# A two-layer streaming encoder: the first MLP's h tiles are issued from ScalarE's queue, and its loads, its side work and the norm behind it are paced differently

## The chip, the core and the metric

The kernel runs on one core of a Trainium2 chip. Its time is the device time of one launch in microseconds (us). Three runs of the kernel before gave 2468.64, 2472.65 and 2472.76 us; the median is 2472.65 us.

The engines are named as in the profile: PE is the matrix engine (TensorE), PEld its weight loads, DVE is VectorE, ACT is ScalarE, POOL is GpSimd, SP is the sync engine, which in this kernel issues the transfers (DMA). An engine works through its own instructions in the order in which they stand, and a transfer is issued when its turn comes on the engine that issues it.

## The reference

One inference step of a two-layer encoder, 1024 prompt tokens and 32 sample tokens side by side (T = 1056), width 1024, float32 throughout:

```
layer 0:  u = x*(1+sc1)+sh1;  y = mLSTM mixer(u);   x = LN(ALPHA*x + (1+g1)*y)
          u = x*(1+sc2)+sh2;  f = square(relu(u @ w_up[0])) @ w_down[0]      # the first MLP, 1024 -> 4096 -> 1024
          x = LN(ALPHA*x + (1+g2)*f)
layer 1:  kv = (x*(1+kv_scale)+kv_shift) @ w_kv;  q = (x*(1+sc1)+sh1) @ w_q
          y = band attention(q, k, v);  x = LN(ALPHA*x + (1+g1)*y);  second MLP;  LN
sh1,sc1,g1,sh2,sc2,g2 of a layer = silu(c) @ w_ada[layer] + b_ada       # "conditioning", 1024 -> 6*1024
kv_shift, kv_scale               = silu(c) @ w_ada_kv + b_ada_kv        # 1024 -> 2*1024
```

The conditioning vectors of layer 1 and of the shared keys and values depend on `c` alone, so they can be computed at any time before the second layer starts.

## The kernel before

Activations stand with features on the partitions and tokens along the free dimension. Every float32 operand of a matmul is split into a rounded part and a remainder: ScalarE casts (`split`, L89), VectorE subtracts (L90), and a product takes three matmuls (L118 to L120, or L1280 in a loop). The 1056 tokens are cut into four quarters of 264 for the up half of the first MLP and into blocks of 384, 384 and 288 (`TBS`) from there on.

**Up half.** `mlp7` with the class `L0` computes `h = square(relu(u @ w_up))` for 16 blocks `pb` of 256 columns. Ten of them (`FIRST`) are computed plainly for the first half of the tokens, while the norm ahead of the MLP still runs. The rest goes in 22 jobs `(pb, tp)` of seven products each (`Seven`, L1280): first blocks with both token halves and blocks with the second half in turn, and at the end five jobs in a row that each bring a new `pb`. For each `pb`, `forms` loads two 128x4x256 tiles `rdn_u` (L1228) and makes eight split operands `wf_u` with sums on VectorE (L1244 to L1247). The result of a job is split into `HL` and stored to the array `hpl` in DRAM (L1147). The loop sorts the products by `7*j+2*i`, and writes TensorE's order out by hand; on the other engines a scheduler places the instructions when the program is built, by its own estimate of when each could start.

**Down half.** Eight groups `g` of 512 rows of `w_down`. A group needs four `h` tiles (`h_load`) and four weight tiles (`w_plain`, 128x4x256 each, load at L96, split at L89 and L90 as `w_dn`), and adds 8 output chunks of 128 columns to the residual `ACX` on VectorE (`add_gated_at`, L1045). The `h` tiles of group 0 are eight strips (L1336) that are loaded into parts of `U` as soon as the last job that reads them is done; those of odd groups are in a pool `f4`, which takes the place of the pool of `H` and `HL`, and those of even groups in `U` again (L1340). The residual comes back from DRAM in four pieces (`reload`, L1620) into two buffers that held operands of the up half.

**Rings.** `raw` has 3 buffers: `rdn_u`, `raw_dn` and the conditioning loads `rada` go through it in turn. `wc` has 6 buffers: `wf_u`, `w_dn` and the wide conditioning loads `radw` go through it.

**Side work.** `Flow` holds generators that compute the conditioning and the norms. Each yields how long to wait, and `tick` counts that down: after each of the seven products by `264/320`, after each output chunk of down by `n/192`. `ada_cols` handles two chunks of 128 columns at a time from two `rada` loads (L231), `ada_wide` four from two `radw` loads (L261), with 16 operations on VectorE per unit of work (L238, L241; L274, L276), two transposes and two sums (L283, L285). During the up half `ada_some` computes all of `w_ada_kv`, during the down half `ada_rest` all of `w_ada[1]` and the table of the attention bias. Behind each block of the last group a norm starts (`norm`: sums L926 to L929, mean and variance on TensorE L923, centring L936, squares L938, L940, scale L951 to L955, modulation L370 to L375), whose result is the operand `U` of the projection `q` (copied out at L1672, L1673). `W01` are the waits between its steps.

## Time and profile before

| | |
|---|---|
| median of 3 runs | 2472.65 us (2468.64 to 2472.76) |
| the profiled execution, its own time | 2473.38 us |
| span of its trace | 2471.5 us |
| mean granted TensorE clock | 0.987 |
| busy: PE, PEld, DVE, ACT, POOL | 96%, 92%, 81%, 48%, 7% of the span |
| chain that ended last | PE 65%, DVE 15%, DMA 8%, ACT 4% |

The up half of the first MLP with its seven products ends at about 887 us of the span, the down half runs from about 881 to 1276 us, and the projection of `q` follows. Rows of the trace give the start in us, the duration in us, the engine, the line, the operation and its tiles; in brackets stands how long the engine stood idle just before, and what ended that. In a table by windows each engine has its busy time and its number of instructions, then come the granted clock of TensorE (1.00 is full speed), the mean busy share of the 16 transfer engines, and GB/s. In a grouped row the count stands after the x, then the busy time and the mean of one in ns, then the idle time before.

### The profile page before, as it was taken

Reading aid. Unit: us, or ns where it says so; the run is one execution under the profiler, and the core shown is the slowest. Engines: PE = TensorE matmul, PEld = TensorE weight load, DVE = VectorE, ACT = ScalarE, POOL = GpSimd, SP = SyncE. Lnnn points to the kernel's source line nnn. Section 1 sums busy time; section 2 is a strip of 40 time slices with the busy share of each in tenths; the row PEclk is TensorE's granted clock in tenths of the full one; section 3 lists DMA queues with packets and bytes.
Section 4 is the critical chain, followed back from the end, with each engine's and each line's share of the span. In section 5 each row is a group of like instructions: output and inputs, shape, how many; then the busy total and the mean of one; then the engine's idle time right before and its main releaser. Section 6 shows DMA issues by size and latency. Waiting matters only on the chain.

```text
span 2471.5 us, 44497 instructions
## 1 busy us (share of the span) xinstructions
PE 2371.9 (96%) x17180; PEld 2273.6 (92%) x17180; DVE 1993.4 (81%) x4254; ACT 1181.9 (48%) x2394; POOL 165.4 (7%) x315
## 2 busy tenths in 40 slices
PE   7999999999999879999999989999999999899997
PEld 4999999999999879999989977789999999899997
DVE  4899899788788889998487666754998888887778
ACT  4544456387566531001047457762776777322212
POOL 0211100000000000000000224420000000000003
PEclk9999999999999989999999999999999999999999
DMA  8433223436566895764422330032476779966642
GB/s 295 124 109 94 84 87 114 131 127 213 185 196 200 286 319 208 259 226 163 152 94 78 83 74 1 10 95 62 138 268 229 255 252 345 372 232 234 230 159 71
DMA packets 294264, 423.62 MB, mean 171 GB/s; under 512 B 15640, under 2 KB 225964, under 8 KB 288932
## 3 DMA queue, kind: packets, MB, share of 16 engines
q1 hardware_dynamic: 294052, 420.78, 50.9%
q8 instruction: 135, 2.21, 0.4%
q14 instruction: 77, 0.63, 0.1%
HBM read 304.91 MB, written 118.17 MB: 171 GB/s over the span
## 4 chain that ended last, share of the span: by engine, by line
PE 65%; DVE 15%; DMA 8%; ACT 4%; issue 3%; POOL 1%; SPq 0%; DVEq 0%; ACTq 0%; POOLq 0%
PE dn L1415 11%; PE up L1280 7%; PE dn L118 5%; PE dn L119 5%; PE dn L120 5%; PE pv L1849 3%; PE s L1792 2%; PE pt L1827 2%; DVE wf_u L90 2%; DMA rdn_u<-in_w_up_dram 2%; PE up L120 2%; PE up L118 2%; PE up L119 2%; DVE HL L90 1%; PE op_a L118 1%
## 5 line engine op out<-in xcount | busy, mean ns | idle before, releaser
L1045 DVE SCALAR_TENSOR_TENSOR ACX<-dn,ada,ACX 128x264 f32<-128x264 f32 (+6 forms) x664 | 281.8, 448 | 115.0 <-PE dn L120 68.6
L1415 PE MATMUL dn<-fx,wf_d 128*128 128x264 f32 x2016 | 254.2, 285 | 6.3 <-DVE ACX L1045 2.8
L1415 PEld LDWEIGHTS dn<-fx,wf_d 128*128 128x128 f32 x2016 | 248.7, 188 | 8.7 <-issue 2.6
L89 ACT CAST w_dn<-raw_dn 128x1024 fp32r<-128x1024 f32 x36 | 37.5, 1050 | 289.9 <-PE dn L120 131.8
L118 PE MATMUL dn<-hs,w_dn 128*128 128x384 f32 (+2 forms) x512 | 161.4, 315 | 0.7 <-DVE ACX L1045 0.7
L120 PE MATMUL dn<-hs,w_dn 128*128 128x384 f32 (+2 forms) x512 | 160.3, 313 | 1.3 <-DVE w_dn L90 1.3
L119 PE MATMUL dn<-hs,w_dn 128*128 128x384 f32 (+2 forms) x512 | 161.0, 315 | 0.0
L1280 PE MATMUL up<-U,wf_u 128*128 128x264 f32 x1056 | 145.8, 290 | 15.8 <-ACT wf_u L89 6.8
L1280 PEld LDWEIGHTS up<-U,wf_u 128*128 128x128 f32 x1056 | 136.2, 192 | 20.4 <-ACT wf_u L89 8.0
L1280 PE MATMUL up<-TF,wf_u 128*128 128x264 f32 x1056 | 142.9, 284 | 0.6 <-ACT H L1283 0.6
L1280 PE MATMUL up<-u,wf_u 128*128 128x264 f32 x1056 | 139.6, 285 | 1.2 <-ACT wf_u L89 0.6
L118 PE MATMUL dn<-U,w_dn 128*128 128x384 f32 (+2 forms) x416 | 130.8, 315 | 10.2 <-ACT w_dn L89 10.0
L1280 PEld LDWEIGHTS up<-TF,wf_u 128*128 128x128 f32 x1056 | 134.3, 188 | 0.9 <-ACT H L1283 0.8
L1280 PEld LDWEIGHTS up<-u,wf_u 128*128 128x128 f32 x1056 | 132.6, 188 | 1.9 <-ACT wf_u L89 0.8
L119 PE MATMUL dn<-U,w_dn 128*128 128x384 f32 (+2 forms) x416 | 130.9, 315 | 0.0
L120 PE MATMUL dn<-U,w_dn 128*128 128x384 f32 (+2 forms) x416 | 129.5, 313 | 0.0
L274 DVE SCALAR_TENSOR_TENSOR aw<-radw,cs,aw 128x512 f32<-128x512 f32 x168 | 118.9, 744 | 0.0
L238 DVE SCALAR_TENSOR_TENSOR ada_room<-ada_room,cs 128x256 f32<-128x256 f32 x224 | 99.7, 479 | 3.5 <-DMA ada_room<-in_w_ada_dram 3.5
L120 PEld LDWEIGHTS dn<-hs,w_dn 128*128 128x128 f32 x512 | 96.4, 188 | 1.7 <-DVE w_dn L90 1.7
L118 PEld LDWEIGHTS dn<-hs,w_dn 128*128 128x128 f32 x512 | 96.3, 188 | 1.1 <-DVE ACX L1045 1.0
L119 PEld LDWEIGHTS dn<-hs,w_dn 128*128 128x128 f32 x512 | 96.5, 188 | 0.0
L120 PE MATMUL up<-u,w_up 128*128 128x264 f32 x320 | 91.8, 288 | 4.2 <-DVE w_up L90 4.2
(394 smaller groups left out, 7187.3 us busy)
## 6 DMA issues: line engine op xcount, KB each, us to landing
hpl<-HL SPq DMA_DIRECT2D x144, 264.0 KB
rdn_u<-in_w_up_dram SPq DMA_DIRECT2D x64, 512.0 KB
hd<-HL SPq DMA_DIRECT2D x28, 1056.0 KB
fx<-hd SPq DMA_DIRECT2D x50, 528.0 KB
radw<-in_w_ada_dram SPq DMA_DIRECT2D x24, 1024.0 KB
hd<-HM SPq DMA_DIRECT2D x28, 792.0 KB
hs<-hpl SPq DMA_DIRECT2D x20, 1056.0 KB
raw_up<-in_w_up_dram SPq DMA_DIRECT2D x40, 512.0 KB
```

The costliest lines, as they stand in the source:

```text
L90: (eng or nc.vector).tensor_sub(dst_l, src, dst_h.bitcast(F32))
L118: nc.tensor.matmul(ps, wh, mov(0, k), start=(k == 0), stop=False)
L119: nc.tensor.matmul(ps, wh, mov(1, k), start=False, stop=False)
L120: nc.tensor.matmul(ps, wl, mov(0, k), start=False, stop=(k == nk - 1))
L238: nc.vector.scalar_tensor_tensor(acc[:, cnd], raw[:, k], sc, acc[:, cnd], op0=ALU.mult, op1=ALU.add)
L274: nc.vector.scalar_tensor_tensor(acc[cnd], raw[:, k], sc, acc[cnd], op0=ALU.mult, op1=ALU.add)
L1045: nc.vector.scalar_tensor_tensor(xs, ps[:, off + o:off + o + mm_], gate[:, fc, cnd:cnd + 1], xs, op0=ALU.mult, op1=ALU.add)
L1280: nc.tensor.matmul(p, self.ws[w][:, wl, k], moving(f, tp, xl, k), start=first and k + n_ == 0, stop=k == 3 and n_ == 2, skip_group_check=n ...
L1415: nc.tensor.matmul(p, ws[w][:, wl, k], t[:, s0, xl], start=first and k + n_ == 0, stop=k == kg - 1 and n_ == 2, skip_group_check=not first)
L1792: nc.tensor.matmul(s[:, b, :w], qst, kk[i][:, g, k0 + j0:k0 + j0 + w], start=(i == 0), stop=(i == 1))
L1827: nc.tensor.transpose(pt[:kp, j - j0, pr * P:(pr + 1) * P], ps_[pr][:, j * P:j * P + kp], ident)
L1849: nc.tensor.matmul(pv[64 * e:64 * e + 64, :nq], V[:kp, vt0 + j, g * 64:(g + 1) * 64], pts[e][:kp, j, :nq], start=(j == 0), stop=(j == nt - 1))
```

## The change

- `h_load` issues the full `h` tiles from ScalarE's queue instead of SP's. The strips stay on SP.
- The strips of group 0 are asked for twice per job (after products 2 and 5) instead of three times, over four jobs instead of three. The residual's pieces 0 and 1 come at job `lone + 5` and at the end of the up half instead of at jobs `lone + 2` and `lone + 3`; pieces 2 and 3 in group 0 instead of at the end of the up half. The `h` tiles of group 1 are asked for one per pair of chunks of group 0 instead of all four ahead of it.
- Conditioning: half of `w_ada_kv` (8 of 16 chunks) moves from `ada_cols` in the up half to `ada_wide` in the down half. The pace in the up half goes from 320 to 480, so the same waits last longer there. In the down half the waits of `ada_wide` go from 5, 5, 2 to 4.5, 4.5, 2, and what a tick overshoots is carried over to the next wait.
- The norm's waits behind the first two blocks get shorter, each block with its own.

```
-    def add(self, gen, wait=0.0, now=False):
-        self.tasks.append([gen, next(gen) if now else wait])
+    def add(self, gen, wait=0.0, now=False, carry=False):
+        self.tasks.append([gen, next(gen) if now else wait, carry])
 ...
-                    t[1] = wait or 0.0
+                    t[1] = (wait or 0.0) + (t[1] if t[2] else 0.0)
 ...
-    ADA_W = (5.0, 5.0, 2.0)
+    ADA_W = (4.5, 4.5, 2.0)
-    W01 = ((6.0, 12.0, 3.0, 3.0, 3.0), (3.0, 6.0, 0.0, 0.0, 0.0))
+    W01 = ((4.0, 6.0, 1.0, 1.0, 1.0), (6.0, 8.0, 2.0, 2.0, 2.0), (3.0, 6.0, 0.0, 0.0, 0.0))
 ...
-            nc.sync.dma_start(t.bitcast(F32), src)
+            nc.scalar.dma_start(t.bitcast(F32), src)
 ...                                                     # up_end
-            L.reload(2)
+            L.reload(2 if NW else 1)
 ...
-                    if i in (2, 4, 6) and not NW and first_h:
+                    if i in (2, 5) and not NW and first_h:
                         h_load(0, *first_h.pop(0))
-                    if i == 0 and j < lone + 4:
+                    if i == 0 and NW and j < lone + 4:
                         L.reload(j - lone - 2)
+                    if i == 0 and not NW and j == lone + 5:
+                        L.reload(0)
 ...
-            L.reload(3)
             L.down()
-            for c in range(4):
-                h_load(1, c)
             for g in range(8):
                 if g < 7:
                     for pr in range(4):
                         w_plain(g, pr)
-                        if g and pr == 0:
+                        if g == 0:
+                            h_load(1, pr)
+                            if pr < 2:
+                                L.reload(2 + pr)
+                        elif pr == 0:
                             for c in range(4):
                                 h_load(g + 1, c)
 ...                                                     # ada_some, ada_rest
-        yield from ada_cols(a["w_ada_kv"], 0, 96, 16, mm, tmp_t, ADA_B)
+        yield from ada_cols(a["w_ada_kv"], 0, 96, 8, mm, tmp_t, ADA_B)
         yield from ada_wide(a["w_ada"][1], 0, 48, 48, mm, tmp_t, wc_tile, ADA_W)
+        yield from ada_wide(a["w_ada_kv"], D, 104, 8, mm, tmp_t, wc_tile, ADA_W)
 ...                                                     # class L0
-        l, nw, pace, alloc, add, gate = 0, 0, 320, mm, add_gated_at, ada_part(0, 5)
+        l, nw, pace, alloc, add, gate = 0, 0, 480, mm, add_gated_at, ada_part(0, 5)
-            norms["ada"] = flow.add(ada_rest())
+            norms["ada"] = flow.add(ada_rest(), carry=True)
 ...
-            norms[ti] = flow.add(norm(ti, 1, f"n01_{ti}", W01[ti == 2], False, lambda ti: acc_dma(
+            norms[ti] = flow.add(norm(ti, 1, f"n01_{ti}", W01[ti], False, lambda ti: acc_dma(
```

TensorE's order in the up half stays as it was; on the other engines the scheduler's order moves, and from the last part of `q` on all orders are the same again. Three places show it. A row gives the line, the operation, the tile written and the tiles read, and the shape. The number at the end of a name only tells tiles of one name apart.

SP's queue where the down half begins, before. `raw_dn_g_i` is the load of weight tile i of group g, `hs_1_c` an h tile of group 1, `radw` a conditioning load, `hpl<-HL` the store of a job's result.

```order
L1147 DMA hpl_6125<-HL_15_1_10414 256x1x264 x4
L261 DMA radw_0_0_10531<-in_w_ada_dram 128x4x512
L261 DMA radw_0_1_10590<-in_w_ada_dram 128x4x512
L1147 DMA hpl_6125<-HL_13_1_10490 256x1x264 x4
L261 DMA radw_4_0_10716<-in_w_ada_dram 128x4x512
L1340 DMA hs_1_0_10509<-hpl_6125 128x2112
L1340 DMA hs_1_1_10511<-hpl_6125 128x2112
L1340 DMA hs_1_2_10513<-hpl_6125 128x2112
L1340 DMA hs_1_3_10515<-hpl_6125 128x2112
L96 DMA raw_dn_0_2_10765<-in_w_down_dram 128x4x256
L96 DMA raw_dn_0_3_10902<-in_w_down_dram 128x4x256
L96 DMA raw_dn_1_0_11031<-in_w_down_dram 128x4x256
```

The four `hs_1` loads stand ahead of weight tiles 2 and 3 of group 0. The same place after the change:

```order
L96 DMA raw_dn_0_2_10663<-in_w_down_dram 128x4x256
L96 DMA raw_dn_0_3_10802<-in_w_down_dram 128x4x256
L1624 DMA ACX_1_10406<-xsp_80 128x2112
L261 DMA radw_0_0_10422<-in_w_ada_dram 128x4x512
L1147 DMA hpl_6125<-HL_15_1_10324 256x1x264 x4
L261 DMA radw_0_1_10467<-in_w_ada_dram 128x4x512
L1624 DMA ACX_1_10406<-xsp_80 128x2112
L1147 DMA hpl_6125<-HL_13_1_10392 256x1x264 x4
L261 DMA radw_4_0_10567<-in_w_ada_dram 128x4x512
L261 DMA radw_4_1_10704<-in_w_ada_dram 128x4x512
L96 DMA raw_dn_1_0_10939<-in_w_down_dram 128x4x256
```

Weight tiles 2 and 3 now stand ahead of the residual's `ACX_1` pieces, of the stores of the last two jobs and of the conditioning loads; no h tile stands on SP's queue.

ScalarE's queue at the same place, before, from the last activation of the up half on:

```order
L1290 ACTIVATE H_13_1_10319<-up_13_1_0_10320 128x264
L1141 ACTIVATE H_13_1_10319<-H_13_1_10319 128x1056
L89 CAST HL_13_1_10490<-H_13_1_10319 128x4x264
L89 CAST w_dn_0_2_10767<-raw_dn_0_2_10765 128x1024
L89 CAST w_dn_0_3_10904<-raw_dn_0_3_10902 128x1024
L89 CAST w_dn_1_0_11033<-raw_dn_1_0_11031 128x1024
L89 CAST w_dn_1_1_11138<-raw_dn_1_1_11136 128x1024
```

ScalarE has nothing but casts of weight tiles there. After the change:

```order
L89 CAST HL_13_1_10392<-H_13_1_10232 128x4x264
L89 CAST w_dn_0_2_10665<-raw_dn_0_2_10663 128x1024
L1340 DMA hs_1_0_10404<-hpl_6125 128x2112
L1340 DMA hs_1_1_10536<-hpl_6125 128x2112
L1340 DMA hs_1_2_10668<-hpl_6125 128x2112
L89 CAST w_dn_0_3_10804<-raw_dn_0_3_10802 128x1024
L1340 DMA hs_1_3_10807<-hpl_6125 128x2112
L89 CAST w_dn_1_0_10941<-raw_dn_1_0_10939 128x1024
L89 CAST w_dn_1_1_11060<-raw_dn_1_1_11058 128x1024
L1340 DMA U<-hpl_6125 128x2112 x4
L89 CAST w_dn_1_2_11169<-raw_dn_1_2_11167 128x1024
L89 CAST w_dn_1_3_11270<-raw_dn_1_3_11268 128x1024
```

The h tiles of group 1 stand between the casts of weight tiles 2 and 3 of group 0, and those of group 2 (into `U`) between the casts of tiles 1 and 2 of group 1. The later groups read alike: four h loads stand between two casts of the group ahead.

VectorE in the last group of the down half, before. `q_n_0`, `qr_n_0` are the sums of squares of the first block's norm, `s_n_1`, `sr_n_1` the sums of the second block's, `dn_7_c_t` is output chunk c at token t.

```order
L1045 SCALAR_TENSOR_TENSOR ACX_1_10487<-dn_7_5_384_13832,ada,ACX_1_10487 128x384
L943 TENSOR_TENSOR q_n_0_13786<-q_n_0_13786 128x384
L1045 SCALAR_TENSOR_TENSOR ACX_1_10487<-dn_7_6_384_13846,ada,ACX_1_10487 128x384
L926 TENSOR_TENSOR s_n_1_13874<-ACX_0_9762 128x768
L90 TENSOR_TENSOR qr_n_0_13801<-q_n_0_13786,qr_n_0_13801 128x384
L1045 SCALAR_TENSOR_TENSOR ACX_1_10487<-dn_7_7_384_13860,ada,ACX_1_10487 128x384
L928 TENSOR_TENSOR s_n_1_13874<-s_n_1_13874,ACX_1_10487 128x768
L1045 SCALAR_TENSOR_TENSOR ACX_0_9762<-dn_7_1_768_13897,ada,ACX_0_9762 128x256
L928 TENSOR_TENSOR s_n_1_13874<-s_n_1_13874,ACX_1_10487 128x768
L1045 SCALAR_TENSOR_TENSOR ACX_0_9762<-dn_7_1_768_13897,ada,ACX_0_9762 128x32
L929 TENSOR_TENSOR s_n_1_13874<-s_n_1_13874 128x384
```

The sums of the second block stand ahead of the first block's variance. The same place after the change:

```order
L90 TENSOR_TENSOR qr_n_0_13747<-q_n_0_13732,qr_n_0_13747 128x384
L1045 SCALAR_TENSOR_TENSOR ACX_1_10406<-dn_7_6_384_13835,ada,ACX_1_10406 128x384
L1045 SCALAR_TENSOR_TENSOR ACX_1_10406<-dn_7_7_384_13858,ada,ACX_1_10406 128x384
L951 SCALAR_TENSOR_TENSOR w_n_0_13795<-var_n_0_13792,w_n_0_13795 128x384
L952 TENSOR_SCALAR w_n_0_13795<-w_n_0_13795 128x384
L953 TENSOR_TENSOR w_n_0_13796<-w_n_0_13795 128x384
L1045 SCALAR_TENSOR_TENSOR ACX_0_10118<-dn_7_0_768_13891,ada,ACX_0_10118 128x256
L955 TENSOR_TENSOR ACX_0_10118<-ACX_0_10118,w_n_0_13796 128x2x384 x2
L955 TENSOR_TENSOR ACX_1_10406<-ACX_1_10406,w_n_0_13796 128x2x384 x2
L375 TENSOR_TENSOR U<-ut_n_0_0_0_13804,U 128x384
```

The first block's scale (`w_n_0`, L951 to L955) and its first modulated chunk follow at once, and the second block's sums come later.

## The prediction

> **What bounds the kernel now.** I read the first part of the page, then TensorE's idle rows in the stretch that the diff touches, then what each was waiting for. Numbers in us.
>
> ```profile
> span 2471.5 us, 44497 instructions
> PE 2371.9 (96%) x17180; PEld 2273.6 (92%) x17180; DVE 1993.4 (81%) x4254; ACT 1181.9 (48%) x2394; POOL 165.4 (7%) x315
> ```
>
> TensorE is busy for 96% of the span, so an edit can win only where TensorE waits or runs at a lowered clock. The table by windows shows where that is around the first MLP:
>
> ```profile
> core 0: us, PE busy (x) PEld busy (x) DVE busy (x) ACT busy (x) POOL busy (x), PEclk, DMA share, GB/s
> 800.00:880.00 80.00, 68.08 (x520) 64.85 (x519) 65.07 (x123) 45.97 (x80) 0.00 (x0) 0.98 0.82 265
> 880.00:910.00 30.00, 27.52 (x228) 26.65 (x226) 26.23 (x57) 6.49 (x9) 0.00 (x0) 1.00 0.99 354
> 910.00:920.00 10.00, 1.39 (x6) 1.29 (x6) 9.07 (x15) 1.98 (x2) 0.00 (x0) 0.54 1.04 382
> 920.00:930.00 10.00, 10.00 (x67) 10.00 (x67) 7.33 (x13) 2.21 (x3) 0.00 (x0) 0.77 0.91 311
> 950.00:1100.00 150.00, 150.00 (x948) 149.15 (x948) 141.18 (x256) 13.68 (x13) 0.00 (x0) 1.00 0.67 242
> 1100.00:1225.00 125.00, 125.00 (x795) 124.15 (x795) 88.28 (x169) 12.99 (x13) 0.00 (x0) 1.00 0.50 174
> 1225.00:1270.00 45.00, 42.95 (x258) 42.31 (x257) 32.38 (x49) 8.95 (x13) 0.00 (x0) 1.00 0.15 47
> 1270.00:1280.00 10.00, 7.86 (x53) 7.30 (x53) 9.66 (x18) 5.79 (x10) 0.00 (x0) 0.98 0.40 133
> 1280.00:1290.00 10.00, 9.04 (x44) 8.72 (x43) 9.55 (x15) 6.99 (x12) 0.00 (x0) 0.85 0.48 151
> 1290.00:1300.00 10.00, 9.39 (x52) 9.02 (x53) 9.18 (x16) 6.14 (x12) 0.00 (x0) 1.00 0.28 88
> 1300.00:1310.00 10.00, 8.63 (x48) 7.76 (x46) 9.15 (x17) 6.83 (x14) 0.00 (x0) 1.00 0.00 1
> 1310.00:1320.00 10.00, 6.95 (x30) 6.44 (x31) 7.73 (x14) 8.66 (x16) 0.00 (x0) 0.83 0.44 157
> ```
>
> From 950 to 1225 TensorE has no idle time and full clock: nothing is to be won there, and only something to be lost. Idle time stands in three places: in the up half, most of it after 800 (80.00 - 68.08 = 11.9 in that row); between 880 and 930; and from 1225 to 1320, where the down half hands over to the norm and `q`. The longest single waits, from TensorE's timeline:
>
> ```profile
> 918.62 0.59 PE L118 MATMUL dn<-U,w_dn 128*128 128x264 f32 x1 [10.03 <-ACT w_dn L89]
> ...
> 1240.57 0.44 PE L120 MATMUL dn<-hs,w_dn 128*128 128x384 f32 x1 [1.34 <-DVE w_dn L90]
> ...
> 1277.44 0.80 PE L118 MATMUL q<-U,w_q 128*128 128x384 f32 x3 [1.75 <-ACT U L370]
> ...
> 1312.55 0.96 PE L118 MATMUL q<-U,w_q 128*128 128x384 f32 x4 [3.81 <-ACT U L370]
> ```
>
> **Term A, the up half.** What TensorE waits for from 800 to 886, in the grouped rows of that window, then for the up half from 690 to 900 on VectorE, and ScalarE's share:
>
> ```profile
> L1280 PE MATMUL up<-U,wf_u 128*128 128x264 f32 x300 | 43.4, 295 | 11.6 <-ACT wf_u L89 6.1 <-DVE H L1286 2.7 <-DVE wf_u L90 2.3
> ```
>
> ```profile
> L1244 DVE TENSOR_TENSOR s_u<-rdn_u,rdn_u 128x512 f32<-128x512 f32 x12 | 8.2, 687 | 9.4 <-DMA rdn_u<-in_w_up_dram 9.4
> ...
> L238 DVE SCALAR_TENSOR_TENSOR aacc<-rada,cs,aacc 128x256 f32<-128x256 f32 x84 | 35.3, 478 | 4.5 <-DMA rada<-in_w_ada_kv_dram 4.5
> ```
>
> The products wait 11.6 for their split weights (`wf_u`) and for VectorE's additions. VectorE waits 9.4 for `rdn_u` to land and spends 35.3 on the conditioning `aacc`, which also holds one or two of the three `raw` buffers through which `rdn_u` comes. The change takes half of `ada_some` out: 8 chunks are four units of 16 operations, and eight of them take 3.26 here:
>
> ```profile
> 878.05 3.26 DVE L238 SCALAR_TENSOR_TENSOR aacc<-rada,cs,aacc 128x256 f32<-128x256 f32 x8 [0.99 <-DMA rada<-in_w_ada_kv_dram]
> ```
>
> So 64 operations, 26 us of VectorE, leave the up half, and at the pace of 480 the eight chunks that stay need about 4 x 13 + 8 = 60 of waits against 154 x 0.55 = 85 of ticks: the conditioning ends around the 16th of 22 jobs. The last five jobs, in which a new weight block comes every seven products, are then free of it, buffers included. I estimate that a quarter of the 11.6 stays, a gain of 8.7. The waits before 800,
>
> ```profile
> L1280 PE MATMUL up<-U,wf_u 128*128 128x264 f32 x480 | 66.1, 290 | 4.2 <-DVE wf_u L90 1.7 <-ACT H L1283 1.1 <-DVE H L1286 0.8
> ```
>
> lie where conditioning goes on as before; the 4.2 stay. One window in the up half shows a lowered clock:
>
> ```profile
> 850.00:860.00 10.00, 6.91 (x40) 6.18 (x41) 8.39 (x14) 6.75 (x11) 0.00 (x0) 0.83 0.66 219
> ```
>
> 6.91 busy at 0.83 is a loss of 1.2, of which I take back 1. **A = 9.7, taken as 10.** The strips and the residual are asked for later, but go through the same full transfer engines (0.82 from 800 to 880), so I give them nothing. Bounds: a third of it, 4, if the transfers were the cause; 15 if nearly every idle row from 690 on goes.
>
> **Term B, the third pair of chunks of group 0.** SP's timeline, then ScalarE's:
>
> ```profile
> 881.33 0.37 SPq L96 DMA_DIRECT2D raw_dn<-in_w_down_dram  x1
> ...
> 899.13 3.15 SPq L1340 DMA_DIRECT2D hs<-hpl  x4
> 902.32 9.29 SPq L96 DMA_DIRECT2D raw_dn<-in_w_down_dram  x3
> ```
>
> ```profile
> 887.01 1.03 ACT L89 CAST w_dn<-raw_dn 128x1024 fp32r<-128x1024 f32 x1
> ...
> 917.52 1.04 ACT L89 CAST w_dn<-raw_dn 128x1024 fp32r<-128x1024 f32 x1 [24.07 <-DMA raw_dn<-in_w_down_dram]
> ```
>
> Weight tile 1 is issued at 881.33 and cast at 887.01, under 6 later. Tile 2 is issued at 902.32, behind four h loads of 1056 KB, which themselves could not start before the pool `f4` was free, and is cast at 917.52; TensorE has stood since 908.6. After the change the two tiles stand ahead of all that on SP's queue. They need a `raw` buffer each, free once the last `wf_u` and `w_dn_0_0` are split, around 884. Even if landing takes the 15.2 of tile 2 here instead of 5.7, the cast ends near 900, against a need at 908.6. The wait of 10.03 goes, and with it the lowered clock behind it: 10.00 busy at 0.77 lose 2.3, and 1.39 at 0.54 lose 0.6. **B = 12.5.** Next in line are the `hs_1` tiles: issued between two casts on ScalarE, the last around 905, they are due at the start of group 1, 931 by then; before, four of them and three weight tiles landed within 18. Bounds: 6, if one of these is late by half the wait; 13.
>
> The Trainium skill, page "TensorE: Matmul & The Clock Gate", Part 1, says that the clock halves only after an idle window of about 3.4 us and comes back after as long a busy one. By that rule only the gap of 10.03 would cost clock, half of 3.4 or 1.7, and A and B would be smaller by 2.2 together. The rows have a lowered clock at 850 to 860 as well, without such a gap, and I keep them.
>
> **Term C, the down half under more conditioning.** A group takes 46.8, from the h loads that SP issues at the start of one odd or even group to the next:
>
> ```profile
> 943.67 2.10 SPq L1340 DMA_DIRECT2D U<-hpl  x4
> ...
> 990.50 2.84 SPq L1340 DMA_DIRECT2D hs<-hpl  x4
> ```
>
> A group has 44 ticks (8 chunks x 1056/192), so a tick is 1.06. VectorE is busy 141.18 of 150 from 950 to 1100. One unit of `ada_wide` has 14 multiply-adds, 2 multiplications, 2 transposes, 2 sums:
>
> ```profile
> 910.63 1.29 DVE L283 STREAM_TRANSPOSE awt<-aw 128x512 f32<-128x512 f32 x2
> 911.85 1.24 DVE L285 TENSOR_REDUCE cx<-awt 128x16 f32<-128x512 f32 x2
> 913.00 0.87 DVE L276 TENSOR_SCALAR aw<-radw,cs 128x512 f32<-128x512 f32 x2
> 913.79 4.06 DVE L274 SCALAR_TENSOR_TENSOR aw<-radw,cs,aw 128x512 f32<-128x512 f32 x6
> ```
>
> 14/6 x 4.06 + 0.87 + 1.29 + 1.24 = 12.9. The window holds 6.4 units:
>
> ```profile
> L274 DVE SCALAR_TENSOR_TENSOR aw<-radw,cs,aw 128x512 f32<-128x512 f32 x90 | 63.9, 744 | 0.0
> ```
>
> (90/14), one in 23.3, which is the 22 ticks of the waits 5, 5, 5, 5, 2. The rest of VectorE's work is 141.18 - 6.43 x 12.9 = 58.2. With 20 ticks, carried exactly, a unit comes every 21.3: 7.05 units, 91.0 + 58.2 = 149.2 of 150. VectorE goes from 0.94 to 0.99. There are 14 units instead of 12, 298 us, up to about 1185, so the norms find it free as before. TensorE waits for VectorE only when eight result banks are full or a weight tile is split late. **C = a loss of 2.** Bounds: 0, since TensorE has no idle time to give there; 8, if VectorE is 1.01 loaded over six groups (2.8) and a few weight tiles come late besides.
>
> ScalarE's 28 h issues cost it about what they cost SP, 2.10 for four above, beside 13.68 busy of 150: nothing on the path. SP no longer stands at a group's start until TensorE frees the tiles; nothing was late for that, so it wins nothing.
>
> **Term D, the norm and `q`.** In the rows from 1270 to 1320 TensorE is idle 2.14 + 0.96 + 0.61 + 1.37 + 3.05 = 8.1, loses 9.04 x 0.15 + 6.95 x 0.17 = 2.5 to the clock, and 2.05 from 1225 to 1270, mostly the late `w_dn` split at 1240.57. The first modulated chunk comes at
>
> ```profile
> 1276.69 0.70 ACT L370 ACTIVATE U<-ACX,comb 128x384 fp32r<-128x384 f32 x1
> ```
>
> after the norm's waits of 6 + 12 ticks. With 4 + 6 it comes 8 ticks, some 8 us, earlier, ahead of the last `down` matmul at 1275.7, so the wait at 1277.44 goes. The wait of 3.81 at 1312.55 is for the second block, whose chain is bounded by VectorE, 9.66, 9.55, 9.18 and 9.15 busy of 10 each. VectorE's work there doesn't shrink; it can only start sooner, in the 45.00 - 32.38 = 12.6 that it is idle from 1225 to 1270. That is enough to take most of it. I leave the split at 1240.57 (1.3) and 4 more. **D = 7.** Bounds: 0, if the second block's sums, which now come later on VectorE, hold TensorE up instead; 11.
>
> **Sum.** 10 + 12.5 - 2 + 7 = 27.5. The profiled execution took 2473.38 (span 2471.5 and 1.9 around it), 0.7 over the median of 2472.65: 2472.65 - 27.5 = **2445**.
>
> **The rivals.**
>
> *VectorE becomes the bound of the down groups.* For it: 0.99, and every result passes through its queue in order. Against it: 0.94 left TensorE without a single wait. It decides once VectorE needs more than 46.8 per group; each 1% over costs 0.47 x 6 = 2.8. At 4% over, 11 more than C: 2456.
>
> *The transfers stay jammed: nothing is really spread.* For it: the transfer share is 0.99, 1.04 and 0.91 from 880 to 930, and the same bytes must come before group 1. Then the gap of B only moves to other tiles (2 left of 12.5), and A keeps 5: 5 + 2 - 2 + 7 = 12, 2461. Against it: the early weight tiles no longer stand behind 4.2 MB. The Trainium skill, page "DMA: Bandwidth & Descriptors", section "Issuing engines are not separate DMA queues", says that issuing from several engines saves only the sequencer's issue time, since all run on the same 16 transfer engines; it speaks for this case, and no row of before shows a second issuing queue.
>
> *ScalarE stands behind its own h loads.* This one ends slower. At each group's start four h loads wait on ScalarE until TensorE has let go of the group before, and the cast of weight tile 2 waits behind them. In the profile that cast comes 12.9 into group 1:
>
> ```profile
> 946.51 1.05 ACT L89 CAST w_dn<-raw_dn 128x1024 fp32r<-128x1024 f32 x1 [11.76 <-DVE aw L274]
> 956.56 1.06 ACT L89 CAST w_dn<-raw_dn 128x1024 fp32r<-128x1024 f32 x1 [8.99 <-PE dn L120]
> ```
>
> It is due before 21 (half a group of 46.8, less a cast of 1.05 and the split). If the loads hold ScalarE until 27, for a buffer or for an earlier transfer, TensorE loses 6 in seven groups, 42: 2472.65 - 27.5 + 42 = 2487. From 25 on it eats the whole gain. Against it: SP got the four loads out within 2.10 and 2.84.
>
> **Chances.** Forecast 0.58 (its own range 2435 to 2452), VectorE-bound 0.14, jammed 0.12, ScalarE's queue 0.11, gains and losses that cancel within 0.2% (4.9 us, about what a measurement of this kernel can tell) 0.05. Faster 0.84, same 0.05, slower 0.11. The range is 2434 (A and D at their upper bounds, C at 0, less a little) to 2466 (jammed, with VectorE 2 worse and A at its lower bound nearly).
>
> **What would show it.** Right: weight tile 2 of group 0 issued before 890 and no idle row of TensorE over 2 in 880 to 935; idle time from 800 to 886 under 5; VectorE near 0.99 from 950 to 1100 and TensorE still above 0.99; `q` starting within 1 of the last `down` matmul. Wrong: a row of TensorE behind `w_dn` or `hs` in groups 1 to 6, a wait on ScalarE of more than 20 at an h load, VectorE at 1.00 with idle rows "<-DVE ACX", or a new wait behind `mean_n` in the last group.

## The result and the profile after

The changed kernel takes 2439.89 us (median of 4 runs, 2437.59 to 2442.02) against 2472.41 for the kernel before (4 runs): a ratio of 0.9872, 95% interval 0.9855 to 0.9889, or 32.5 us less. The forecast was 2445, with a range of 2434 to 2466. Times differ by some 4 us from one group of runs to the next, for both kernels alike, so every run below stands beside runs of before on the same chip. The two profiled executions, 2437.59 and 2473.38, are 35.8 apart. First the profile's page, span and engines:

```profile
span 2435.8 us, 44452 instructions
PE 2363.6 (97%) x17180; PEld 2265.8 (93%) x17180; DVE 1987.5 (82%) x4222; ACT 1178.8 (48%) x2394; POOL 166.6 (7%) x315
```

The same windows as in the prediction; the number behind an engine's busy time counts its instructions:

```profile
690.00:800.00 110.00, 107.21 (x867) 105.66 (x866) 89.72 (x164) 69.32 (x122) 0.00 (x0) 1.00 0.62 200
800.00:880.00 80.00, 78.92 (x650) 78.18 (x649) 59.50 (x103) 48.01 (x81) 0.00 (x0) 1.00 0.93 316
880.00:910.00 30.00, 29.68 (x243) 29.47 (x243) 28.87 (x57) 3.15 (x3) 0.00 (x0) 1.00 0.94 344
910.00:920.00 10.00, 10.00 (x70) 9.71 (x69) 9.67 (x20) 0.81 (x1) 0.00 (x0) 1.00 0.92 357
950.00:1100.00 150.00, 148.85 (x937) 146.13 (x936) 144.64 (x258) 14.10 (x14) 0.00 (x0) 1.00 0.63 227
1100.00:1225.00 125.00, 122.97 (x759) 121.36 (x758) 101.12 (x192) 16.19 (x18) 0.00 (x0) 1.00 0.52 182
1225.00:1270.00 45.00, 39.98 (x232) 38.34 (x231) 41.34 (x71) 24.98 (x41) 0.00 (x0) 0.93 0.26 82
```

From 800 to 880 TensorE is now idle for 1.1 instead of 11.9, although the transfer engines are busier there (0.93 against 0.82). The gap at 910 is gone. From 950 to 1225, where it had no idle time, it now has some. The places in between are best fixed by three rows of TensorE's timeline, the first product of group 1, of group 7 and of `kv`. Before:

```profile
944.69 0.33 PE L118 MATMUL dn<-hs,w_dn 128*128 128x384 f32 x1
...
1225.43 0.34 PE L118 MATMUL dn<-hs,w_dn 128*128 128x384 f32 x1
...
1382.52 0.28 PE L1742 MATMUL kv<-w_kv,uk 128*128 128x256 f32 x1
```

After:

```profile
910.78 0.34 PE L118 MATMUL dn<-hs,w_dn 128*128 128x384 f32 x1
...
1195.35 0.34 PE L118 MATMUL dn<-hs,w_dn 128*128 128x384 f32 x1
...
1348.84 0.28 PE L1746 MATMUL kv<-w_kv,uk 128*128 128x256 f32 x1
```

For the up half I counted its 1848 products in TensorE's timeline (line 1280) backwards from the last one: from the 1824th-last to the 36th-last product it takes 878.8 - 636.4 = 242.4 before and 858.2 - 634.4 = 223.8 after. With that the spans divide as follows:

| stretch | before | after | gained |
|---|---|---|---|
| up to the 1824th-last product of the up half | 636.4 | 634.4 | 1.9 |
| up half from there (A) | 242.4 | 223.8 | 18.6 |
| on to the start of group 1 (B) | 65.9 | 52.6 | 13.3 |
| groups 1 to 6 (C) | 280.7 | 284.6 | -3.8 |
| group 7 to the first product of `kv` (D) | 157.1 | 153.5 | 3.6 |
| the rest | 1089.0 | 1087.0 | 2.0 |

A to D make 31.7, close to the 32.5 between the medians. The first and the last line lie where the diff changes nothing; in the other profiles the first point varies between 633.4 and 635.3, before's is the latest.

### The profile page after: what moved, and what is told of

Its sections match the earlier page's. It is cut to its first block, busy times and chain, and to the rows that moved or that the text cites. A ratio compares the mean times of both kernels' runs of the same rounds, so it can differ in the third digit from the quotient of the medians.

```text
span 2435.8 us, 44452 instructions
## 1 busy us (share of the span) xinstructions
PE 2363.6 (97%) x17180; PEld 2265.8 (93%) x17180; DVE 1987.5 (82%) x4222; ACT 1178.8 (48%) x2394; POOL 166.6 (7%) x315
## 4 chain that ended last, share of the span: by engine, by line
PE 47%; DVE 12%; DMA 5%; ACT 4%; issue 2%; POOL 1%; SPq 0%; DVEq 0%; ACTq 0%; POOLq 0%
PE dn L1415 11%; PE up L1280 9%; PE dn L120 5%; PE dn L119 5%; PE dn L118 5%; PE pv L1853 3%; PE s L1796 2%; PE pt L1831 2%; DMA rdn_u<-in_w_up_dram 1%; DVE wf_u L90 1%; PE op_b L118 1%; PE op_b L119 1%; PE op_b L120 1%; DVE HL L90 1%; DMA radw<-in_w_ada_dram 1%
## 5 line engine op out<-in xcount | busy, mean ns | idle before, releaser
L120 PE MATMUL dn<-hs,w_dn 128*128 128x384 f32 (+2 forms) x512 | 155.9, 314 | 1.8 <-DVE w_dn L90 1.8
L1280 PE MATMUL up<-U,wf_u 128*128 128x264 f32 x1056 | 139.6, 285 | 1.6 <-DVE H L1286 1.0
L274 DVE SCALAR_TENSOR_TENSOR aw<-radw,cs,aw 128x512 f32<-128x512 f32 x196 | 139.5, 745 | 0.0
L119 PE MATMUL dn<-U,w_dn 128*128 128x384 f32 (+2 forms) x416 | 129.8, 313 | 0.0
L118 PE MATMUL dn<-U,w_dn 128*128 128x384 f32 (+2 forms) x416 | 129.3, 311 | 0.0
L120 PE MATMUL dn<-U,w_dn 128*128 128x384 f32 (+2 forms) x416 | 125.6, 312 | 0.9 <-DVE w_dn L90 0.9
L120 PEld LDWEIGHTS dn<-hs,w_dn 128*128 128x128 f32 x512 | 95.8, 188 | 2.9 <-DVE w_dn L90 2.6
L1806 DVE CUSTOM_DVE_ANT_0 p<-s,bias 128x576 f32<-128x576 f32 (+9 forms) x132 | 79.1, 606 | 20.3 <-PE s L1796 13.4
```

What stands on the lines that cost most here:

```text
L118: nc.tensor.matmul(ps, wh, mov(0, k), start=(k == 0), stop=False)
L119: nc.tensor.matmul(ps, wh, mov(1, k), start=False, stop=False)
L120: nc.tensor.matmul(ps, wl, mov(0, k), start=False, stop=(k == nk - 1))
L274: nc.vector.scalar_tensor_tensor(acc[cnd], raw[:, k], sc, acc[cnd], op0=ALU.mult, op1=ALU.add)
L1280: nc.tensor.matmul(p, self.ws[w][:, wl, k], moving(f, tp, xl, k), start=first and k + n_ == 0, stop=k == 3 and n_ == 2, skip_group_check=n ...
L1806: nc.vector.tensor_tensor_reduce(out=z.rearrange("p (b w) -> p b w", b=np_), in0=s[:, :np_, :w], in1=bt.rearrange("p (b w) -> p b w", b=np ...
```

## The experiments

Twelve runs in three groups. "Gain" is the median of before in the same group less the run's; the ratio has its 95% interval.

| run | what it is | median | gain | ratio |
|---|---|---|---|---|
| e1_cond | before + conditioning | 2441.96 | 27.4 | 0.9895 [0.9877, 0.9912] |
| e2_spread | before + spread loads | 2467.84 | 1.5 | 0.9993 [0.9984, 1.0003] |
| e3_queue | before + h tiles from ScalarE | 2474.82 | -5.4 | 1.0021 [1.0010, 1.0031] |
| e4_w01 | before + norm waits | 2464.26 | 5.1 | 0.9982 [0.9973, 0.9991] |
| x1_vec | VectorE's work kept in the up half, loads gone | 2449.76 | 20.5 | 0.9917 [0.9897, 0.9937] |
| x2_load | loads kept, VectorE's work gone | 2460.72 | 9.6 | 0.9969 [0.9959, 0.9979] |
| m3_noqueue | after, h tiles on SP | 2435.04 | 35.3 | 0.9862 [0.9846, 0.9878] |
| m2_nospread | after without the spreading | 2438.40 | 31.9 | 0.9877 [0.9858, 0.9895] |
| c0_after | after once more | 2435.03 | 33.3 | 0.9866 [0.9853, 0.9880] |
| a475 | after, waits 4.75 | 2429.22 | 39.1 | 0.9844 [0.9830, 0.9857] |
| b475 | a475, h tiles on SP | 2430.27 | 38.1 | 0.9846 [0.9832, 0.9860] |
| b50 | b475, waits 5 | 2432.12 | 36.2 | 0.9857 [0.9843, 0.9872] |

**One part at a time.** The conditioning alone, with `ADA_W`, the carry and the pace of 480 as in the change:

```
-        yield from ada_cols(a["w_ada_kv"], 0, 96, 16, mm, tmp_t, ADA_B)
+        yield from ada_cols(a["w_ada_kv"], 0, 96, 8, mm, tmp_t, ADA_B)
         yield from ada_wide(a["w_ada"][1], 0, 48, 48, mm, tmp_t, wc_tile, ADA_W)
+        yield from ada_wide(a["w_ada_kv"], D, 104, 8, mm, tmp_t, wc_tile, ADA_W)
...
-        l, nw, pace, alloc, add, gate = 0, 0, 320, mm, add_gated_at, ada_part(0, 5)
+        l, nw, pace, alloc, add, gate = 0, 0, 480, mm, add_gated_at, ada_part(0, 5)
```

> The kernel before with the conditioning part alone: half of w_ada_kv moved to the down half, pace 480, waits 4.5, 4.5, 2, carried. Loads stay on SP in their old places in the code. In the changed kernel's profile the up half is 18.6 us shorter from 690 on, the first group of down 13.3, the later groups together 3.8 longer. Theory (side work): the up half waits because the conditioning holds VectorE and the raw buffers; the whole 18.6 comes with this part alone. The scheduler here also puts weight tiles 2 and 3 of group 0 ahead of the h loads, so the 13.3 come too, and the 3.8 are paid: 2472.4 - 18.6 - 13.3 + 3.8 = 2444. Rival (transfers): the up half waits because strips and residual fill the transfer engines; then this part gives at most 5 there, and the time is 2457 or more. A second rival (SP held): from group 1 on, weight tile 1 now stands behind h loads on SP that wait for the group ahead to end; if it then lands 3 us late in each of seven groups, 21 are given back: 2465, with waits of TensorE for w_dn early in each group.

It gains 27.4. The up half, counted as above, takes 221.8, so the whole of A is in it, and group 1 starts at 909.40: B as well, with the h loads still on SP. Group 1 is 2.1 longer than in the changed kernel (958.91 - 909.40 = 49.5 against 47.4), the later ones are alike, so the second rival is right for one group and not for seven. The transfers' rival falls: strips and residual are as before here.

The spreading alone, with the reloads as in the change:

```
-                    if i in (2, 4, 6) and not NW and first_h:
+                    if i in (2, 5) and not NW and first_h:
...
-            for c in range(4):
-                h_load(1, c)
...
+                            h_load(1, pr)
```

> The kernel before with the spreading alone: strips twice per job over four jobs, residual pieces later, h tiles of group 1 one per pair of chunks of group 0, all still on SP. Side-work theory: the up half keeps its waits (0 to 2 us gained); in group 0 weight tile 2 stands behind two h loads instead of four, 2.1 MB less at about 350 GB/s, so some 6 of the gap of 10 go: 2464 to 2469. Transfer theory: the up half loses most of its waits, 15 us, and the gap goes as well: 2447 to 2452.

The up half takes 241.7, as before within 1, and half of the gap stays:

```profile
910.29 0.59 PE L118 MATMUL dn<-U,w_dn 128*128 128x264 f32 x1 [5.27 <-ACT w_dn L89]
```

This is the expectation of the side-work theory in both places. By the medians little of it is left: 1.5, with an interval that includes no gain at all.

The queue alone:

```
-            nc.sync.dma_start(t.bitcast(F32), src)
+            nc.scalar.dma_start(t.bitcast(F32), src)
```

> The kernel before with the full h tiles issued from ScalarE's queue, and nothing else. Side-work theory: the up half keeps its waits. Weight tile 2 of group 0 no longer stands behind the four h loads; it is issued about 3 us earlier and lands in some 6 us instead of 15 if the h loads start behind it: the gap of 10 shrinks to between 0 and 5, 2459 to 2467. Rival (one set of transfer engines): the h loads start at the same time from the other queue and share the engines with it; the gap stays within 2 of 10, 2470 to 2473. Rival (ScalarE held): ScalarE stands at the h loads until their buffers are free, casts behind them come late, and the later groups get waits for w_dn: above 2475.

The edit that the change is named after makes the kernel slower, by 0.2%. SP's row where weight tile 2 of group 0 goes out, then TensorE's rows with the longest waits:

```profile
900.28 5.00 SPq L96 DMA_DIRECT2D raw_dn<-in_w_down_dram  x3
```

```profile
917.45 0.59 PE L118 MATMUL dn<-U,w_dn 128*128 128x264 f32 x1 [8.87 <-ACT w_dn L89]
...
1104.33 0.41 PE L118 MATMUL dn<-U,w_dn 128*128 128x384 f32 x1 [1.99 <-DVE ACX L1045]
...
1150.59 0.66 PE L118 MATMUL dn<-hs,w_dn 128*128 128x384 f32 x1 [3.46 <-DVE ACX L1045]
```

Next come SP's rows just ahead of the second of VectorE's longest waits, and then those two waits:

```profile
1124.13 9.85 SPq L96 DMA_DIRECT2D raw_dn<-in_w_down_dram  x2
1137.30 0.37 SPq L261 DMA_DIRECT2D radw<-in_w_ada_dram  x1
```

```profile
1103.14 0.49 DVE L276 TENSOR_SCALAR aw<-radw,cs 128x512 f32<-128x512 f32 x1 [7.41 <-DMA radw<-in_w_ada_dram]
...
1149.14 0.75 DVE L274 SCALAR_TENSOR_TENSOR aw<-radw,cs,aw 128x512 f32<-128x512 f32 x1 [10.26 <-DMA radw<-in_w_ada_dram]
```

Weight tile 2 is issued at 900.28 instead of 902.32, and the gap is 8.87 instead of 10.03: the h loads ahead of it were not what held its issue, since it stands behind the stores and the conditioning loads as well. Nor does it land sooner: it is cast at 916.35, 16.1 after its issue, where before took 15.2. The gap stays within 2 of 10, as the rival of one set of transfer engines had it. In the later groups neither expected thing happens. ScalarE stands idle for up to 9.4 ahead of an h load (until 941.28 and until 988.10), but TensorE has no wait for a cast there. But with the h loads off SP the scheduler puts weight tiles ahead of conditioning loads there, these land late, VectorE stands at them for 7.41 and 10.26, the additions to `ACX` wait behind in its queue, and then TensorE waits for these. Groups 4 and 5 take 50.6 and 52.9 (1082.67, 1133.27, 1186.21) instead of 46.8.

The norm's waits alone:

```
-    W01 = ((6.0, 12.0, 3.0, 3.0, 3.0), (3.0, 6.0, 0.0, 0.0, 0.0))
+    W01 = ((4.0, 6.0, 1.0, 1.0, 1.0), (6.0, 8.0, 2.0, 2.0, 2.0), (3.0, 6.0, 0.0, 0.0, 0.0))
```

> The kernel before with the shorter waits of the norm behind the first two blocks, and nothing else. In the changed kernel's profile the stretch from the start of the last group to the first product of kv is 3.6 us shorter. Theory: that comes from these waits alone, 2469, with q starting before the last product of down. Rival: VectorE's load there sets the time whatever the order, 2472, and the 3.6 come with something else.

5.1 by the medians; from group 7 to `kv` 1377.13 - 1224.88 = 152.3 against 157.1. The norm's waits alone carry D. Added up, the two runs' gains of 27.4 and 5.1 are the 32.5 of the whole change.

**Which resource the conditioning held.** x1_vec has the 8 moved chunks' operations on a resident tile in the up half, x2_load their loads and four operations of 16 columns on each; the moved chunks are computed in the down half as after the change, with its waits, and the pace is 320:

```
+        yield from ada_busy(104, 8, tmp_t, ADA_B)
...
+                            nc.vector.scalar_tensor_tensor(acc[:, cnd], acc[:, cnd], cs[:, k, cnd:cnd + 1], acc[:, cnd],
+                                                           op0=ALU.mult, op1=ALU.add)
```

```
+        yield from ada_hold(a["w_ada_kv"], D, 104, 8, tmp_t, ADA_B)
...
+                    nc.vector.tensor_scalar(acc[:, half, 16 * k:16 * k + 16], raw[:, k, 0:16], cs[:, 0, 0:1], None,
+                                            op0=ALU.mult)
```

> The kernel before with half of w_ada_kv moved to the down half, waits 4.5, 4.5, 2 carried, pace 320 as before; and in the up half, where chunks 8 to 15 of the conditioning stood, the same number of multiply-adds, transposes and sums on VectorE on a resident tile, without the loads. So VectorE carries before's work up to the end of the up half, and the raw buffers and transfers are free of it. Measured from product 0 to product 1800 of the up half: 240.9 us before, 220.3 with the conditioning part alone. If VectorE's time was the cause: 235 or more and a total above 2455. If the raw buffers and loads were the cause: under 226 and a total of 2440 to 2448. On SP the weight tiles 2 and 3 of group 0 stand ahead of the h loads here; so no gap in group 0 by either theory.

> The counterpart: in the up half chunks 8 to 15 are loaded into the raw buffers as before and held as long, but VectorE only reads 16 columns of each, so its time for them is nearly gone. If the raw buffers and loads were the cause of the up half's waits: 234 or more from product 0 to 1800, and a total of 2465 to 2475, since weight tile 2 of group 0 again waits for a raw buffer and stands behind the h loads on SP, with the gap of about 10. If VectorE's time was the cause: under 226, and 2450 to 2458 with the gap alone.

Up half, counted as in the table of stretches: 242.4 with both, 230.5 with the loads, 224.9 with VectorE's work, 221.8 without either (e1_cond, which also has the pace of 480). Taking the loads away gains 17.5, taking VectorE's time away 11.9; together only 20.6, so part of the waits needed both at once. The raw buffers and loads are the larger part; these runs don't separate the held buffer from the transfer itself. Both totals lie between what the two theories expected, 2449.76 against 2440 to 2448 or above 2455, and 2460.72 against 2465 to 2475 or 2450 to 2458. Nor did x2 come up to the 234 expected from product 0 to 1800: it has 232.0, where the trace of before has 243.9 by that count, not the 240.9 of the expectation. Each kernel's longest wait in group 0, x2 first, then x1:

```profile
905.16 0.59 PE L118 MATMUL dn<-U,w_dn 128*128 128x264 f32 x1 [10.95 <-ACT w_dn L89]
```

```profile
894.69 0.59 PE L120 MATMUL dn<-U,w_dn 128*128 128x264 f32 x1 [5.34 <-DVE w_dn L90]
```

With the loads held in `raw`, the whole gap of B is back: tiles 2 and 3 stand behind the h loads on SP again. Without them that wait is gone, and the tiles stand ahead. x1 has another wait of half its size, for a split on VectorE, which neither theory expected and which costs it most of its difference from e1_cond. So B, too, hangs on the conditioning's loads, and by the order on SP on the `raw` buffer that they hold. In before, SP's waits from 878 to 905 show it being held at weight tile 1 (us in total, times, longest):

```profile
SPq L96 <- DVE aacc L238: 1.9, 1, 1.9
```

**The changed kernel without a part.**

> The changed kernel with the h tiles issued from SP again, all else as changed. If ScalarE's queue is what the change needs beside the conditioning (in the run with the conditioning alone the groups 1 and 2 of down were 2.7 us longer, with tiles behind h loads on SP): slower than the changed kernel by 2 to 6, 2442 to 2446. If, as alone, the queue costs time: faster by up to 4, 2436 to 2439.

> The changed kernel with strips, residual and the h tiles of group 1 at their old places in the code (h tiles still from ScalarE's queue). Theory: the spreading is worth nothing here, as alone (ratio 0.9993): 2437 to 2442. Rival: with the h tiles of group 1 all issued at once from ScalarE they hold it or crowd the weight tiles of group 0, and a gap of 2 to 6 comes: 2442 to 2446.

The queue is worth nothing that these runs can tell: m3's 2435.04 looked like a gain over 2439.89, but the changed kernel itself, run again, gave 2435.03. The spreading stays open. By the gains m2 is 1.4 behind the changed kernel run again, and its time is inside what was expected without an effect. But in its one profile the rival shows too: group 0 takes 51.3 (862.28 to 913.56), against 46.8 in m3 and in c0_after and 47.4 in the changed kernel's first profile, with waits and a clock of 0.94 from 880 to 910:

```profile
888.39 0.39 PE L118 MATMUL dn<-U,w_dn 128*128 128x264 f32 x1 [1.07 <-DVE ACX L1045]
890.05 0.49 PE L120 MATMUL dn<-U,w_dn 128*128 128x264 f32 x1 [0.56 <-DVE w_dn L90]
```

**The six groups.** The changed kernel again, and then with longer waits of the wide conditioning:

> The changed kernel itself once more, as the neighbour for the three that follow: 2437 to 2442.

```
-    ADA_W = (4.5, 4.5, 2.0)
+    ADA_W = (4.75, 4.75, 2.0)
```

> The changed kernel with the waits of the wide conditioning at 4.75, 4.75, 2: a unit in 21 ticks instead of 20. With 4.5 the groups 1 to 6 of down take 284.6 us together against 280.7 before; but in the run that only held the buffers the same conditioning at 4.5 took 281.2, with VectorE as busy, and there the scheduler had kept TensorE's products chunk by chunk. In the changed kernel it had mixed the products of neighbouring chunks (a product with the remainder of a weight tile comes after the next chunk's first ones); with 4.75 it doesn't. Theory (order): the six groups return to 281, 3 to 4 us less, 2436. Rival (VectorE's load): 5% fewer conditioning operations per group give back 1 to 2: 2438 to 2439.

Groups 1 to 6 take 281.2, from these rows, against 1193.51 - 908.95 = 284.6 in c0_after:

```profile
909.68 0.34 PE L118 MATMUL dn<-hs,w_dn 128*128 128x384 f32 x1
...
1190.89 0.34 PE L118 MATMUL dn<-hs,w_dn 128*128 128x384 f32 x1
```

Of the 3.8 lost in these groups 3.4 is back, as the order theory had it. The windows from 950 to 1100 of a475 and of x2_load, which has the waits of 4.5 as the changed kernel:

```profile
950.00:1100.00 150.00, 150.00 (x955) 148.95 (x954) 144.31 (x257) 13.93 (x14) 0.00 (x0) 1.00 0.63 228
```

```profile
950.00:1100.00 150.00, 150.00 (x950) 149.24 (x949) 144.75 (x257) 13.67 (x13) 0.00 (x0) 1.00 0.64 231
```

VectorE is as busy in all three (144.31, 144.75, 144.64); TensorE issues 955, 950 and 937 products. What differs is the order of these. In the changed kernel the scheduler writes, where group 4 begins,

```
L118 MATMUL dn_3_7_768_12242<-hs_3_0_11388,w_dn_3_3_12158 128x288
L119 MATMUL dn_3_7_768_12242<-hs_3_0_11388,w_dn_3_3_12158 128x288
L118 MATMUL dn_4_0_0_12270<-U,w_dn_4_0_12259 128x384
L119 MATMUL dn_4_0_0_12270<-U,w_dn_4_0_12259 128x384
L118 MATMUL dn_4_0_384_12288<-U,w_dn_4_0_12259 128x384
L119 MATMUL dn_4_0_384_12288<-U,w_dn_4_0_12259 128x384
L120 MATMUL dn_3_6_0_12161<-hs_3_0_11388,w_dn_3_3_12158 128x384
```

the first products of several chunks ahead of the first product with a weight tile's remainder (L120); in a475, x2_load and before each piece is finished in turn in these groups. The other profiles agree: m3, m2, x1_vec and e1_cond, with mixed products, take 284.2 to 285.7 for the six groups; b475 and b50, without, 281.2 and 280.7. In the changed kernel the remainder is also late when it runs, from 950 to 1100 at two places:

```profile
1032.22 0.45 PE L120 MATMUL dn<-hs,w_dn 128*128 128x384 f32 x1 [0.45 <-DVE w_dn L90]
...
1079.68 0.44 PE L120 MATMUL dn<-U,w_dn 128*128 128x384 f32 x1 [0.59 <-DVE w_dn L90]
```

They are a quarter of the loss; the rest lies in pauses too short for a row. VectorE's order changes with TensorE's, and no run changes one without the other. Why the scheduler's estimate of that remainder is late in the one kernel and not in the other stays open. a475 is 5.8 faster than c0_after, with runs of 2428.85 to 2431.14 against 2434.14 to 2435.88: it beats both kernels, and the gain is more than the 3 to 4 expected. The two profiles are 4.4 apart, so 1 to 2.4 are not placed.

> The same with the h tiles on SP again. If the ScalarE queue costs what it did in the two runs where it was alone or taken away (+5, -5 between calls): 2431 to 2434. If that was the difference between calls: as the one ahead, 2436.

> The same as the one ahead with 5, 5, 2 carried: a unit in 22 ticks, so 14 units take 308 ticks, exactly the seven groups ahead of the last one. The six groups stay at 281. If the last unit runs into the norm of the first block, 1 to 4 more than the one ahead; otherwise the same, 2431 to 2436.

b475 is no different from a475 that these runs can tell: here the queue costs nothing, and gives nothing. In b50 the groups stay at 280.7 (907.65 to 1188.37), but from group 7 to `kv` it takes 155.5 against 152.7 in b475, with one long wait for the second block's norm; by the medians, 2432.12 against 2430.27, the two can't be told apart:

```profile
1249.19 1.28 PE L923 MATMUL var_n<-qr_n,ones_d 128*128 128x384 f32 x2 [7.46 <-ACT qr_n L89]
```

## Why the prediction was right, and where it wasn't

The forecast was 5 above the result, inside its range, by terms that erred both ways: A 10 against 18.6, B 12.5 against 13.3, C -2 against -3.8, D 7 against 3.6. That it came so close is partly luck: the 8.6 too little in A was offset by the 5.2 too much in C and D.

**A: the right cause, mis-sized, outside its bounds of 4 to 15.** Three steps failed. Two are "a quarter of the 11.6 stays" and "the 4.2 stay": idle time from 690 to 880 went from 4.2 + 11.9 to 2.8 + 1.1. The third is that idle time isn't the whole loss. At full pace the up half starts 82 products in 10 us; the changed kernel shows it, in a row whose 84 include two that began before it:

```profile
820.00:830.00 10.00, 10.00 (x84) 10.00 (x84) 7.91 (x15) 5.84 (x12) 0.00 (x0) 1.00 1.06 354
```

From 800 to 880 before's 520 hold 517 that start there, work for 63.0, in 68.1 of busy time: some 5 were lost in time that counts as busy, about 1.5 of it by the lowered clock from 856 to 860 (rows in the last section) and the rest, by my estimate, around the waits. They come on top of the 11.9 of idle time. After, 639 full products and 8 small ones leave some 2 lost in all. The row stood in the prediction; I read its busy time and not its count.

**B: right in size and in the order on SP's queue, but not in what brings that order about.** The weight tiles are issued early and the wait is gone:

```profile
856.29 1.31 SPq L96 DMA_DIRECT2D raw_dn<-in_w_down_dram  x2
```

```profile
872.89 1.05 ACT L89 CAST w_dn<-raw_dn 128x1024 fp32r<-128x1024 f32 x1
```

The prediction had tile 2 "behind four h loads" and its cast, after the change, ending near 900; it came at 872.89. e1_cond has B with all h loads on SP, while e3_queue, with all of them gone from there, has 2.7 of its 13.3: what moves the tiles is the conditioning that gives back a `raw` buffer.

**C: the loss was within its bounds, its main cause wrong.** VectorE came to 144.64 of 150, not to 149.2, and x2_load shows that such a load by itself costs nothing. The loss goes with the order that the scheduler wrote, which the prediction didn't look at in the groups. It did name weight tiles split late as one way to lose, and "a row of TensorE behind `w_dn`" in groups 1 to 6 as a sign of being wrong: the rows at 1032.22 and 1079.68 are that sign, if a small one.

**D: both waits that it named are gone, a new one takes half.** `q` starts at 1243.63, ten ahead of the last product of down at 1253.4, and the waits of 1.75 and 3.81 are away. Instead TensorE now stands for a late split of `w_q` and, earlier than before, for the second block's norm:

```profile
1250.37 0.44 PE L120 MATMUL q<-U,w_q 128*128 128x384 f32 x1 [1.32 <-DVE w_q L90]
...
1262.38 0.44 PE L923 MATMUL var_n<-qr_n,ones_d 128*128 128x384 f32 x1 [2.05 <-ACT qr_n L89]
1263.68 0.69 PE L923 MATMUL var_n<-qr_n,ones_d 128*128 128x384 f32 x1 [0.86 <-DVE qr_n L90]
1265.03 0.66 PE L118 MATMUL q<-U,w_q 128*128 128x384 f32 x1 [0.66 <-DVE QO L1677]
```

The norm's wait was the reason given for the lower bound of 0 ("the second block's sums, which now come later"). From 1225 to 1320 TensorE now loses 5.1 to idle time and some 3 to the clock (rows in the last section), where the prediction left 5.3 in all: that is most of what D lacks.

**The rivals.** The VectorE-bound and the jammed transfers did not come: 0.93 to 0.94 of the transfer engines were busy from 800 to 910 with hardly a wait of TensorE. The Trainium skill, page "DMA: Bandwidth & Descriptors", section "Issuing engines are not separate DMA queues", has a second issuing engine save issue time alone; a475 and b475 agree, 2429.22 and 2430.27. ScalarE did stand ahead of its h loads, as that rival said, but for 9.1 at most, not past the point where a cast was due: no wait of TensorE in groups 1 to 6 is for ScalarE. The longest lasts from the end of a cast at 995.50 to the loads at 1004.56:

```profile
994.45 1.05 ACT L89 CAST w_dn<-raw_dn 128x1024 fp32r<-128x1024 f32 x1 [10.62 <-PE dn L120]
1004.56 2.39 ACTq L1340 DMA_DIRECT2D U<-hpl  x4
```

The queue's harm in e3_queue took another way.

## What to carry over

Size a stall by the products issued in its window against the pace of an undisturbed one, not by idle time: here the count gave 17 lost where the idle time gave 11.9. Side work in a shared ring of three buffers can cost more through its loads and the buffers that they hold than through its engine time, here 17.5 against 11.9, and it also decides where a scheduler puts the loads behind it; try each part of a change alone before crediting the one in its name. After every change of pacing look at the order of the bounding engine too: a quarter of a tick in a wait was worth 5.8 us.

## What the runs showed of the hardware

The clock was lowered to about half after waits of 2 to 3 us. In windows of 2 us, before, and then the changed kernel around the norm:

```profile
854.00:856.00 2.00, 0.00 (x0) 0.00 (x0) 1.45 (x3) 1.10 (x2) 0.00 (x0) 1.00 0.08 27
856.00:858.00 2.00, 1.59 (x6) 1.29 (x7) 2.00 (x4) 1.00 (x3) 0.00 (x0) 0.57 0.47 159
858.00:860.00 2.00, 2.00 (x12) 2.00 (x12) 2.00 (x4) 1.90 (x4) 0.00 (x0) 0.58 0.99 301
```

```profile
1260.00:1262.00 2.00, 0.33 (x2) 0.01 (x1) 1.97 (x4) 0.66 (x2) 0.00 (x0) 1.00 0.00 0
1262.00:1264.00 2.00, 0.76 (x2) 0.47 (x2) 1.97 (x4) 0.80 (x2) 0.00 (x0) 0.90 0.68 195
1264.00:1266.00 2.00, 1.34 (x4) 1.00 (x4) 1.91 (x4) 0.00 (x0) 0.00 (x0) 0.50 0.19 68
1266.00:1268.00 2.00, 2.00 (x8) 2.00 (x7) 1.87 (x5) 1.59 (x4) 0.00 (x0) 0.50 0.00 0
1268.00:1270.00 2.00, 2.00 (x8) 2.00 (x8) 0.97 (x2) 1.43 (x3) 0.00 (x0) 0.50 0.00 0
```

In before one wait of 2.62 is followed by some 4 us at about half clock. After the change no wait there is over 2.05, but TensorE is busy for 1.09 of the 4 us from 1260 to 1264, and the clock is 0.50 for the 6 us from 1264: about 3 more lost, nearly as much as the waits. The Trainium skill, page "TensorE: Matmul & The Clock Gate", Part 1, speaks of an idle window of about 3.4 us; here 2.62 of idle, or a few products in 4 us, were enough. The length of a wait alone doesn't settle it. In x2_load a wait of 2.05 that ends at 862.79 left the clock at 1.00; in e3_queue one of 1.99 that ends at 1104.33 was followed by a lowered one, as the rows show, x2_load first:

```profile
862.00:864.00 2.00, 1.21 (x10) 1.24 (x11) 1.88 (x8) 0.00 (x0) 0.00 (x0) 1.00 0.99 345
864.00:866.00 2.00, 2.00 (x19) 2.00 (x18) 0.24 (x1) 1.32 (x2) 0.00 (x0) 1.00 1.02 318
```

```profile
1104.00:1106.00 2.00, 1.67 (x7) 1.70 (x8) 2.00 (x6) 0.00 (x0) 0.00 (x0) 0.71 0.14 50
1106.00:1108.00 2.00, 2.00 (x8) 2.00 (x7) 2.00 (x4) 0.00 (x0) 0.00 (x0) 0.50 0.00 0
```
